# The weighted sum over heads in a prompt indexer: VectorE additions by head, or a second float32 matmul in four column strips

## The chip, the cores and the metric

One Trainium2 chip, one of its cores. The metric is the device time of one execution of the whole program in microseconds (us), the median of several runs. One further execution was taken by the hardware profiler, and all rows below come from it.

## The reference

Two layers of a streaming encoder run on 512 prompt tokens and 32 sample tokens. Each layer projects its normed input with one combined matrix, runs three mixers, an output projection and a feed-forward network. Mixer C is a sparse attention: an indexer scores every key for each query, the best k keys are kept, and attention runs over those. The indexer, cut from the reference:

```python
logits = relu(einsum('bqnd,bsd->bqns', qi, ki_all))
iscore = einsum('bqn,bqns->bqs', wi, logits)
iscore = where(admissible, iscore, -inf)
_, sel = top_k(iscore, k_top)
```

There are n = 8 indexer heads of 32 features. `wi` holds a weight for each query token and head. For the prompt the queries come in blocks of 128 tokens; a block sees the keys up to its own chunk of 64 tokens.

## The kernel before, in words

Features are split over partitions and tokens lie along the free axis, in two halves (256 prompt tokens; 256 prompt and 32 sample tokens). Large products are made exact enough from three float32r products of split operands (`mm3`, L225 to L227). Weights come in by DMA and are split by ScalarE (L216) and VectorE or GpSimd (L217). Some products of the sample's 32 rows are true float32 (L377): eight pieces of the contraction, four of them side by side in strips of 32 columns of the array, which `sum4` (L370) adds up afterwards.

A layer's mixer C begins with the indexer, `for b in range(5)`, L494 to L581. Blocks b = 0 to 3 are the prompt's, b = 4 is the sample. Each block's projection comes from `tok_gemm` (L497); L396, L398 and L509 apply the rotary factors, L508 keeps the eight weights per token in `wi`. The key part is split in two (L516, L518), transposed and appended to `kiTp` (L522). The query part is split (L530, L532), transposed (L103, the one line of all transposes) and copied to `qiT` (L540), so that one matmul of 128 contraction rows gives a head's float32-like scores.

For prompt blocks b = 1 to 3 (n = 256, 384, 512 keys) the loop over heads is:

```python
for hd in range(8):
    pl = psum("lld"[hd % 3])
    nc.tensor.matmul(pl[:, :n], lhsT=qiT[:, hd, :], rhs=kiTp[:, :n], start=True, stop=True)
    rl = T(n, "tt")
    nc.scalar.activation(rl, pl[:, :n], AF.Relu)
    if hd == 0:
        nc.vector.tensor_scalar(work, rl, wi[:, 0:1], None, op0=ALU.mult)
    else:
        nc.vector.scalar_tensor_tensor(work, rl, wi[:, hd:hd + 1], work, op0=ALU.mult, op1=ALU.add)
```

These are L544 (TensorE), L546 (ScalarE), L548 and L550 (VectorE). L551 masks the later chunk. The sample block does the same with a second matmul: L576 gives scores of four heads times 32 tokens, L579 sums them over heads with a float32 matrix `wsel` that L561 and L570 build from `wi`.

Behind the indexer come the q, k and v projections with rotary factors and norms (L597, L622, L641; the key's norm is L644 to L648, its transposes go through L103), the top-k selection of the prompt blocks on VectorE (`topk_mask`, L405 and L406, 16 rounds a block), the search for the sample's threshold (`sample_mask`, L431 to L443) and attention (L689 and on).

The order of each engine is set by a scheduler: instructions have priorities in the order in which they are traced (shifted for weight loads and copies out of PSUM, class `Shift`), and each engine then takes its instructions strictly in the order so found. Gemm matmuls of other products are laid between the indexer's steps in this way; they are called fillers here.

Of the kernel before, what the change touches and what calls it, by code (L numbers as in the profile page):

```python
# [25 lines left out]
# column groups of w_in  # L26
# [5 lines left out]
# scheduling priorities of weight loads and of copies out of PSUM  # L32
PREP = -1000000
EVAC = -2000000
# columns of the ring of split weights
# [3 lines left out]
class Shift:  # L39
    """Shifts the scheduling priority of what is traced inside."""  # L40
# [12 lines left out]
def kernel(  # L53
# [39 lines left out]
    def psum(tag):  # L93
        return pp.tile([128, 512], F32, tag=tag, name=nm("ps" + tag), bufs=PBUFS[tag])
# [4 lines left out]
    def tr(out, in_, ident):  # L99
        """A transpose on TensorE, which moves the bits as they are (float32r in one pass)."""  # L100
        if in_.dtype == F32R:
            out = out.bitcast(F32R)
        nc.tensor.transpose(out, in_, ident)  # L103
# [20 lines left out]
    # per-feature vectors as columns: g_mix, g_ffn, conv_w, state_conv  # L124
# [23 lines left out]
    def rsqrt_newton(r, s, scale, shape_like):  # L148
        """r = (s * scale) ** -0.5, the table's value with one Newton step; s may lie in PSUM."""
# [9 lines left out]
    def take_x(h, tags):  # L159
        """A half of x to feature-major, and the norm's factors along the rows' columns."""  # L160
# [34 lines left out]
    for g in range(4):  # L195
        nc.vector.tensor_copy(sum4[32 * g:32 * g + 32, 96:128], idn[32 * g:32 * g + 32, 32 * g:32 * g + 32])
    p = psum("o")
# [4 lines left out]
    ring = [wp.tile([128, RING], F32R, name="hi"), wp.tile([128, RING], F32R, name="lo"), 0]  # L202

    def load_w(fill, a, c, eng=None):
        """a row blocks of weights, c columns each: two float32r parts that sum to them exactly, and they themselves."""
# [24 lines left out]
    # the sample's normed rows, not split  # L230
    hraw = const.tile([128, 8, 32], F32, name="hraw")

    def add_square(h, m):
        """Adds the squares of block m of x to the half's sum (with the eps share of a partition)."""
# [29 lines left out]
    def results(b, g, tag):  # L264
        """A block's output, half of its features, back to token-major."""
# [15 lines left out]
    def prepare(l):  # L281
# [42 lines left out]
    def search_constants():  # L324
# [3 lines left out]
        # for the threshold search: prefix sums, the copies' total, steps  # L328
# [15 lines left out]
    for l in range(depth):  # L344
# [20 lines left out]
        def tok_gemm(b, pieces, n, aside=True):  # L365
            """Token-major product of a block; aside: the sample's rows by themselves, in float32."""
# [5 lines left out]
            if b == 0 and aside:  # L372
                # the sample's rows: parts of the sum side by side in the array's columns
# [17 lines left out]
        def rope(t1, t2, x, ca, sb, half):  # L391
            """t1 = x * cos, t2 = swapped x * sin; x [rows, j, h, e] in PSUM."""
# [8 lines left out]
        def topk_mask(work, n, rounds, tag):  # L401
            """Turns scores into 0 where taken and NEG elsewhere."""
# [6 lines left out]
        def sample_mask(x):  # L409
            """The same for the sample's scores, whose rows are there four times (rows 32 j + t).  # L410

            The k-th largest score is found digit by digit (two bits of its float's exponent or mantissa at a
            time, each copy of a row trying one digit); equal scores are taken in the order of the keys.
            """
# [4 lines left out]
            # sign of the k-th largest; which one of sgn * x it is  # L419
# [7 lines left out]
            def digit(nb):  # L427
                """How many candidates of a row at least kk of sgn * x reach (a tie at the candidate counts half)."""
# [29 lines left out]
            # a tie at the last candidate may have hidden it: count exactly there  # L458
# [10 lines left out]
            # prefix counts of the equal ones  # L469
# [8 lines left out]
            # as many of them as are missing: k - (sum of signs + n - equal) / 2  # L478
# [15 lines left out]
        for b in range(5):  # L494
# [38 lines left out]
            if b < 4:  # L533
                n = 128 * (b + 1)
                qiT = Q([128, 8, 128], F32R)
                for g in range(2):
                    pt = psum("l")
                    for k in range(4):
                        tr(pt[:, k * 128:k * 128 + 128], qs[:, 4 * g + k].rearrange("p a e -> p (a e)"), idr)
                    nc.scalar.copy(qiT[:, 4 * g:4 * g + 4, :].rearrange("p h t -> p (h t)"), pt)  # L540
                work = keep([128, n], f"work{b}")
                for hd in range(8):
                    pl = psum("lld"[hd % 3])
                    nc.tensor.matmul(pl[:, :n], lhsT=qiT[:, hd, :], rhs=kiTp[:, :n], start=True, stop=True)  # L544
                    rl = T(n, "tt")
                    nc.scalar.activation(rl, pl[:, :n], AF.Relu)  # L546
                    if hd == 0:
                        nc.vector.tensor_scalar(work, rl, wi[:, 0:1], None, op0=ALU.mult)  # L548
                    else:
                        nc.vector.scalar_tensor_tensor(work, rl, wi[:, hd:hd + 1], work, op0=ALU.mult, op1=ALU.add)  # L550
                nc.vector.memset(work[0:64, n - 64:n], INADM)  # L551
                masks[b] = work
            else:
# [5 lines left out]
                # w as two [(head, t), (copy, t)] matrices  # L559
# [47 lines left out]
        for u in range(2):  # L607
            pieces = w_tok(C_Q + 256 * u, 256, ((0, 4), (4, 8)), nc.gpsimd)
            for b in range(5):
# [5 lines left out]
                # columns (j, hh, e) to (hh, j, e)  # L615
# [63 lines left out]
        def attend(b):  # L679
            """The block's steps of a pair of query heads: scores and softmax, then the values."""  # L680
# [3 lines left out]
            def scores(u, hh):  # L684
                # two key heads side by side: their scores in halves of the array's rows
# [21 lines left out]
            def values(u, hh, probs, po):  # L707
                for k0 in range(0, b + 1, 2):
# [7 lines left out]
                    # and their values in halves of its columns  # L716
# [16 lines left out]
        def attend_sample():  # L733
# [17 lines left out]
            # queries, scaled  # L751
# [293 lines left out]
```

## Time and profile before

| what | value |
|---|---|
| median of 3 runs | 1400.68 us (1397.32 to 1401.14) |
| the profiled execution, its span | 1403.4 us |
| TensorE busy | 1353.1 us, 96% |
| VectorE busy | 840.0 us, 60% |
| ScalarE busy | 615.9 us, 44% |
| GpSimd busy | 115.3 us, 8% |

For the profiled execution the page gives the span and no other time. Busy shares are means over the whole span; the windows below show stretches of ten microseconds, in which an engine that is busy for 10.00 has no gap. PE is TensorE, DVE VectorE, ACT ScalarE, POOL GpSimd. In a row of the timeline, "[2.42 <-ACT t L546]" says that the engine was idle for 2.42 us before, and that ScalarE's instruction of line 546, which writes a tile named t, released it. A float32 matmul leaves two records, so that x16 of L377 are eight matmuls. PEclk is the clock that TensorE was granted, 1.00 being full speed.

### The profile page before, as it was taken

The page shows a single profiled execution, that of the slowest core. Times are in us where ns is not written, and L with a number is a line of the kernel's source. Part 1 is how long each engine was busy: PE and PEld are TensorE (multiplying, and loading weights), DVE is VectorE, ACT ScalarE, POOL GpSimd, SP SyncE. Part 2 cuts the span into 40 slices and gives each one's busy share as a digit, 9 for nine tenths or more (in the row PEclk, how much of TensorE's full clock was granted, in tenths as well). Part 3 has the DMA queues.
Part 4 walks back from the last instruction along what each step waited for, and adds up shares of the span by engine and source line. Part 5 has one row for each costly group of instructions (what it writes and reads, how often), then busy time and mean ns, then how long its engine had stood idle before and what let it go on. Part 6 is the DMA issues. An engine that isn't in the chain of part 4 may idle for free. (4 is left out here: it accounts for less than half of the span.)

```text
span 1403.4 us, 25751 instructions
## 1 busy us (share of the span) xinstructions
PE 1353.1 (96%) x10430; PEld 1265.8 (90%) x10430; DVE 840.0 (60%) x2103; ACT 615.9 (44%) x1212; POOL 115.3 (8%) x125
## 2 busy tenths in 40 slices
PE   7998999998999999999989899999899999999998
PEld 5877886898999999999987789779799999999998
DVE  6999987468434334334489999865853343443442
ACT  5746996335314224223246489842542231331321
POOL 4414200010000000000042120000200000000000
PEclk8999999999999999999988999999999999999999
DMA  7124221323233332333212222222233332233322
GB/s 185 33 71 106 68 64 48 94 68 89 81 88 91 91 84 84 89 91 91 64 49 62 58 81 77 76 61 61 61 95 88 91 91 86 82 90 91 91 81 74
DMA packets 183566, 113.00 MB, mean 81 GB/s; under 512 B 7028, under 2 KB 180616, under 8 KB 183448
## 3 DMA queue, kind: packets, MB, share of 16 engines
q1 hardware_dynamic: 180808, 106.35, 26.2%
q0 software_dynamic: 2640, 5.01, 1.8%
q8 instruction: 82, 1.34, 0.4%
q14 instruction: 36, 0.29, 0.1%
HBM read 106.67 MB, written 4.67 MB: 79 GB/s over the span
## 5 line engine op out<-in xcount | busy, mean ns | idle before, releaser
L216 ACT CAST hi<-raw 128x1024 fp32r<-128x1024 f32 (+1 forms) x188 | 194.1, 1032 | 404.6 <-PE psm L226 389.1
L217 DVE TENSOR_TENSOR lo<-raw,hi 128x1024 fp32r<-128x1024 f32 (+1 forms) x163 | 197.5, 1212 | 174.9 <-ACT hi L216 174.2
L908 DVE TENSOR_TENSOR x<-x,psm 128x256 f32<-128x256 f32 (+1 forms) x192 | 83.7, 437 | 232.4 <-PE psm L227 232.0
L226 PE MATMUL psm<-h1lo,hi 128*128 128x288 f32 x640 | 190.4, 298 | 0.9 <-DVE h1lo L222 0.9
L227 PE MATMUL psm<-a1hi,lo 128*128 128x288 f32 x640 | 190.0, 297 | 0.0
L226 PE MATMUL psm<-a1lo,hi 128*128 128x288 f32 x640 | 189.9, 297 | 0.0
L225 PE MATMUL psm<-a1hi,hi 128*128 128x288 f32 x640 | 189.8, 297 | 0.0
L225 PE MATMUL psm<-h1hi,hi 128*128 128x288 f32 x640 | 188.7, 296 | 1.1 <-ACT h1hi L221 1.1
L227 PE MATMUL psm<-h1hi,lo 128*128 128x288 f32 x640 | 189.1, 296 | 0.0
L226 PE MATMUL psm<-h0lo,hi 128*128 128x256 f32 x640 | 181.9, 285 | 6.2 <-DVE h0lo L222 6.2
L225 PE MATMUL psm<-a0hi,hi 128*128 128x256 f32 x640 | 183.0, 286 | 0.0
L226 PE MATMUL psm<-a0lo,hi 128*128 128x256 f32 x640 | 182.0, 284 | 0.0
L227 PE MATMUL psm<-a0hi,lo 128*128 128x256 f32 x640 | 182.0, 284 | 0.0
L225 PE MATMUL psm<-h0hi,hi 128*128 128x256 f32 x640 | 181.4, 284 | 0.0
L227 PE MATMUL psm<-h0hi,lo 128*128 128x256 f32 x640 | 180.0, 282 | 0.0
L226 PEld LDWEIGHTS psm<-h0lo,hi 128*128 128x128 f32 x640 | 120.4, 188 | 8.6 <-DVE h0lo L222 7.1
L225 PEld LDWEIGHTS psm<-h1hi,hi 128*128 128x128 f32 x640 | 120.1, 188 | 2.7 <-ACT h1hi L221 1.5
L225 PEld LDWEIGHTS psm<-a0hi,hi 128*128 128x128 f32 x640 | 121.6, 190 | 0.5 <-issue 0.5
L226 PEld LDWEIGHTS psm<-h1lo,hi 128*128 128x128 f32 x640 | 120.3, 188 | 1.8 <-DVE h1lo L222 1.3
L226 PEld LDWEIGHTS psm<-a0lo,hi 128*128 128x128 f32 x640 | 121.2, 189 | 0.6 <-issue 0.5
L225 PEld LDWEIGHTS psm<-h0hi,hi 128*128 128x128 f32 x640 | 120.6, 189 | 1.2 <-issue 0.9
L227 PEld LDWEIGHTS psm<-a0hi,lo 128*128 128x128 f32 x640 | 121.6, 190 | 0.0
(318 smaller groups left out, 2841.1 us busy)
## 6 DMA issues: line engine op xcount, KB each, us to landing
raw<-in_w_up_dram SPq DMA_DIRECT2D x64, 512.0 KB, 4.1
raw<-in_w_down_dram SPq DMA_DIRECT2D x64, 512.0 KB, 3.9
raw<-in_w_in_dram SPq DMA_DIRECT2D x36, 512.0 KB, 3.9
raw<-in_w_out_dram SPq DMA_DIRECT2D x8, 512.0 KB, 3.8
raw<-in_w_out_dram SPq DMA_DIRECT2D x32, 128.0 KB, 3.0
raw<-in_w_in_dram SPq DMA_DIRECT2D x8, 296.0 KB, 6.1
q<-in_cache_k_dram SPq DMA_DIRECT2D x4, 512.0 KB, 4.3
h1lo<-in_cache_v_dram SPq DMA_DIRECT2D x2, 1024.0 KB, 7.1
```

The lines of the kernel that those rows point to most:

```text
L216: nc.scalar.copy(hi, raw)
L217: (eng or nc.vector).tensor_tensor(lo, raw, hi.bitcast(F32), op=ALU.subtract)
L225: nc.tensor.matmul(out, lhsT=st[0], rhs=mv[0], start=first, stop=False)
L226: nc.tensor.matmul(out, lhsT=st[0], rhs=mv[1], start=False, stop=False)
L227: nc.tensor.matmul(out, lhsT=st[1], rhs=mv[0], start=False, stop=last)
L908: nc.vector.tensor_tensor(xs[h][:, m, :], xs[h][:, m, :], p[:, :HALF[h]], op=ALU.add)
```

## The change

The 128 query tokens of a prompt block are taken as four quarters of 32. A score matmul now has four heads times 32 tokens as its output rows, like the sample's, so there are still eight a block (two groups of heads g, four quarters q4). The weighted sum over heads is a float32 matmul with a 128 × 32 matrix of weights `wst` for each g and q4, which writes the quarter's 32 rows of one PSUM tile (tag "o", one buffer); the two groups accumulate. ScalarE copies the sum to `work`. `wst` is made by GpSimd (weights times a matrix of stacked identities, `fold`), two float32 transposes and a copy. The lines behind move by 5 to 21: L544 becomes L564, L546 L566, L551 L572, L579 L600, L225 to L227 become L230 to L232, L377 L382, L509 L514, L518 L523, L532 L537, L396 L401, L405 L410, L406 L411.

```diff
+    fold = const.tile([128, 32], F32, name="fold")
+    nc.vector.memset(fold, 0.0)
+    for g in range(4):
+        nc.vector.tensor_copy(fold[32 * g:32 * g + 32], idn[32 * g:32 * g + 32, 32 * g:32 * g + 32])
...
-                qiT = Q([128, 8, 128], F32R)
+                qiT = Q([128, 2, 4, 4, 32], F32R)
...
-                    nc.scalar.copy(qiT[:, 4 * g:4 * g + 4, :].rearrange("p h t -> p (h t)"), pt)
+                    nc.scalar.copy(qiT[:, g].rearrange("p q h t -> p h q t"), pt.rearrange("p (h q t) -> p h q t", h=4, q=4))
+
+                dg = T(256)
+                nc.gpsimd.tensor_tensor(
+                    dg.rearrange("p (h t) -> p h t", h=8),
+                    wi.rearrange("p (h o) -> p h o", o=1).to_broadcast([128, 8, 32]),
+                    fold.rearrange("p (o t) -> p o t", o=1).to_broadcast([128, 8, 32]), op=ALU.mult)
+                wst = T(256)
+                pt = psum("l")
+                for g in range(2):
+                    tr(pt[:, g * 128:g * 128 + 128], dg[:, g * 128:g * 128 + 128], idn)
+                nc.scalar.copy(wst, pt[:, :256])
+
                 work = keep([128, n], f"work{b}")
-                for hd in range(8):
-                    pl = psum("lld"[hd % 3])
-                    nc.tensor.matmul(pl[:, :n], lhsT=qiT[:, hd, :], rhs=kiTp[:, :n], start=True, stop=True)
-                    rl = T(n, "tt")
-                    nc.scalar.activation(rl, pl[:, :n], AF.Relu)
-                    if hd == 0:
-                        nc.vector.tensor_scalar(work, rl, wi[:, 0:1], None, op0=ALU.mult)
-                    else:
-                        nc.vector.scalar_tensor_tensor(work, rl, wi[:, hd:hd + 1], work, op0=ALU.mult, op1=ALU.add)
+                pi = psum("o")
+                for g in range(2):
+                    rls = []
+                    for q4 in range(4):
+                        pl = psum("lld"[(4 * g + q4) % 3])
+                        nc.tensor.matmul(pl[:, :n], lhsT=qiT[:, g, q4].rearrange("p h t -> p (h t)"), rhs=kiTp[:, :n], start=True, stop=True)
+                        rl = T(n, ("tt", "tt", "pt", "g")[q4])
+                        nc.scalar.activation(rl, pl[:, :n], AF.Relu)
+                        rls.append(rl)
+                    for q4 in range(4):
+                        c = g * 128 + 32 * q4
+                        nc.tensor.matmul(pi[32 * q4:32 * q4 + 32, :n], lhsT=wst[:, c:c + 32], rhs=rls[q4], start=(g == 0), stop=(g == 1))
+                nc.scalar.copy(work, pi[:, :n])
                 nc.vector.memset(work[0:64, n - 64:n], INADM)
```

The change also moves instructions, since the scheduler sets the order anew. The first place is TensorE in block 1 of layer 0, among the score matmuls (q is `qiT`, psm the gemm's sum). Before:

```order
L225 MATMUL psm_888<-hi,h0hi_184 128x256
L544 MATMUL psl_506<-kiTp_325,q_487 128x256
L226 MATMUL psm_888<-lo,h0hi_184 128x256
L544 MATMUL psl_516<-kiTp_325,q_487 128x256
L227 MATMUL psm_888<-hi,h0lo_185 128x256
L225 MATMUL psm_888<-hi,h0hi_184 128x256
L226 MATMUL psm_888<-lo,h0hi_184 128x256
L544 MATMUL psl_521<-kiTp_325,q_487 128x256
L227 MATMUL psm_888<-hi,h0lo_185 128x256
L225 MATMUL psm_888<-hi,h0hi_184 128x256
```

With the change, from the third score matmul of the block on (pso is the new sum, its t operands are a Relu's output and `wst`):

```order
L564 MATMUL psl_527<-kiTp_331,q_493 128x256
L570 MATMUL pso_514<-t_517,t_508 32x256
L570 MATMUL pso_514<-t_521,t_508 32x256
L570 MATMUL pso_514<-t_525,t_508 32x256
L564 MATMUL psl_535<-kiTp_331,q_493 128x256
L570 MATMUL pso_514<-t_529,t_508 32x256
L564 MATMUL psl_543<-kiTp_331,q_493 128x256
L230 MATMUL psm_921<-hi,h0hi_190 128x256
L231 MATMUL psm_921<-lo,h0hi_190 128x256
L232 MATMUL psm_921<-hi,h0lo_191 128x256
```

Score matmuls and fillers now alternate with the new products, three of which stand together and the fourth behind a further score matmul. The transposes of key block 0 in layer 0, further on, have 31 gemm matmuls between themselves and the transposes ahead of them, where they had 24; in layer 1 both orders have 24.

The second place is VectorE from the sample block's L509 (now L514) on, in layer 0. Before:

```order
L509 TENSOR_TENSOR t_771<-t_771,t_772 32x288
L548 TENSOR_SCALAR work_100_500<-t_503,wi_93_467 128x256
L550 SCALAR_TENSOR_TENSOR work_100_500<-t_508,wi_93_467,work_100_500 128x256
L550 SCALAR_TENSOR_TENSOR work_100_500<-t_513,wi_93_467,work_100_500 128x256
L550 SCALAR_TENSOR_TENSOR work_100_500<-t_518,wi_93_467,work_100_500 128x256
L518 TENSOR_TENSOR ks_576<-t_567,ks_576 128x32 x2
L550 SCALAR_TENSOR_TENSOR work_100_500<-t_523,wi_93_467,work_100_500 128x256
L532 TENSOR_TENSOR q_584<-t_567,q_584 128x8x32
L550 SCALAR_TENSOR_TENSOR work_100_500<-t_528,wi_93_467,work_100_500 128x256
L532 TENSOR_TENSOR q_584<-t_567,q_584 128x8x32
```

With the change:

```order
L514 TENSOR_TENSOR t_804<-t_804,t_805 32x288
L523 TENSOR_TENSOR ks_591<-t_582,ks_591 128x32 x2
L537 TENSOR_TENSOR q_599<-t_582,q_599 128x8x32 x2
L572 MEMSET work_103_513 64x64
L410 MAX m_489_1997<-work_103_513 128x8
L401 TENSOR_TENSOR t_946<-psm_921,tab_76_418 128x2x2x64
L403 TENSOR_TENSOR t_947<-psm_921,tab_77_421 128x2x2x32 x2
L523 TENSOR_TENSOR ks_702<-t_693,ks_702 128x32 x2
L643 TENSOR_TENSOR t_946<-t_946,t_947 128x256
L411 MATCH_REPLACE work_103_513<-m_489_1997,work_103_513 128x256
```

The steps of block 2 (its ks and q) follow the sample's addition at once, and the top-k selection of block 1 (MAX, MATCH_REPLACE) begins here, where before the additions of `work` stand. Where the key's norm begins, block 1 has had 16 rounds of its selection, where it had 7, and block 2 has had 10, where it had 4.

## Rows read from the trace of the kernel before

**Rows 1.** The page, busy time, share of the span and instructions of each engine.

```profile
PE 1353.1 (96%) x10430; PEld 1265.8 (90%) x10430; DVE 840.0 (60%) x2103; ACT 615.9 (44%) x1212; POOL 115.3 (8%) x125
```

**Rows 2.** Windows: each engine's busy us (instructions), TensorE's granted clock, DMA share, GB/s.

```profile
50.00:60.00 10.00, 8.04 (x49) 7.55 (x50) 8.81 (x25) 6.62 (x20) 3.06 (x3) 0.83 0.19 54
60.00:70.00 10.00, 9.88 (x70) 8.80 (x69) 9.22 (x24) 9.08 (x21) 0.00 (x0) 1.00 0.01 2
70.00:80.00 10.00, 8.07 (x55) 5.93 (x54) 9.48 (x21) 3.87 (x11) 2.36 (x1) 0.85 0.33 100
100.00:110.00 10.00, 8.37 (x71) 8.20 (x71) 9.89 (x36) 3.12 (x8) 3.16 (x2) 1.00 0.37 126
110.00:120.00 10.00, 7.60 (x64) 6.48 (x62) 9.91 (x41) 4.39 (x10) 3.96 (x4) 0.90 0.44 133
740.00:750.00 10.00, 8.44 (x57) 8.12 (x57) 9.08 (x20) 7.58 (x22) 3.01 (x3) 0.87 0.36 107
760.00:770.00 10.00, 8.40 (x61) 7.05 (x61) 9.71 (x22) 4.78 (x11) 2.36 (x1) 0.83 0.35 107
790.00:800.00 10.00, 8.00 (x68) 7.82 (x67) 9.93 (x35) 2.88 (x7) 2.95 (x2) 1.00 0.23 66
800.00:810.00 10.00, 7.68 (x62) 6.49 (x61) 9.57 (x40) 4.67 (x10) 3.47 (x3) 0.88 0.46 140
```

**Rows 3.** TensorE's timeline, layer 0: start, us, instruction, [idle before <-releaser].

```profile
51.42 0.39 PE L544 MATMUL psl<-kiTp,q 128*128 128x256 f32 x1 [2.42 <-ACT t L546]
...
73.97 0.98 PE L103 MATMUL psl<-idr,q 32*128 32x32 f32 x10 [1.44 <-ACT t L546]
```

**Rows 4.** TensorE's timeline, layer 1, same columns.

```profile
736.77 0.58 PE L544 MATMUL psl<-kiTp,q 128*128 128x256 f32 x1 [2.04 <-ACT q L540]
...
737.74 1.94 PE L377 MATMUL psm<-raw,hraw 128*32 128x256 f32 x16
...
766.29 0.31 PE L103 MATMUL psl<-idr,q 32*128 32x32 f32 x2 [1.11 <-DVE q L561]
```

**Rows 5.** All engines' timeline, 47.8 to 51.0 us, same columns.

```profile
47.80 2.38 POOL L217 TENSOR_TENSOR lo<-raw,hi 128x1024 fp32r<-128x1024 f32 x1
...
47.93 2.57 DVE L509 TENSOR_TENSOR t<-t,t 32x288 f32<-32x288 f32 x1
...
50.98 0.39 ACT L546 ACTIVATE t<-psl 128x256 f32<-128x256 f32 x1 [2.58 <-DVE work L548]
```

**Rows 6.** VectorE's instructions by line: count, busy us, mean ns, idle before.

```profile
L550 DVE SCALAR_TENSOR_TENSOR work<-t,wi,work 128x256 f32<-128x256 f32 (+2 forms) x42 | 31.3, 746 | 1.3 <-DVE wsel L570 0.3
...
L548 DVE TENSOR_SCALAR work<-t,wi 128x256 f32<-128x256 f32 (+2 forms) x6 | 2.4, 396 | 0.1
```

**Rows 7.** Waits of TensorE: total us, times, longest us.

```profile
PE psx L103 <- DVE sr L644: 3.6, 2, 2.0
```

**Rows 8.** TensorE's timeline, 111.9 to 113.8 us.

```profile
111.93 0.28 PE L227 MATMUL psm<-hi,h1lo 128*128 128x256 f32 x1
112.05 0.38 PE L103 MATMUL psx<-idr,t 128*128 128x128 f32 x2
112.27 0.60 PE L370 MATMUL psm<-t,sum 128*128 128x256 f32 x2
112.79 1.07 PE L377 MATMUL psm<-raw,hraw 128*32 128x256 f32 x16
113.80 0.18 PE L433 MATMUL psd<-ti,rsum 128*128 128x1 bf16 x1
```

**Rows 9.** TensorE's timeline, 770.3 to 771.4 us: the sample's indexer.

```profile
770.29 1.02 PE L579 MATMUL psl<-t,wsel 128*128 128x512 f32 x2
770.75 0.80 PE L576 MATMUL psl<-kiTs,new 128*128 128x512 f32 x1
771.38 0.38 PE L103 MATMUL psd<-idr,t 128*128 128x128 f32 x2
```

**Rows 10.** ScalarE's Relus of the indexer by line (three widths).

```profile
L546 ACT ACTIVATE t<-psl 128x256 f32<-128x256 f32 (+2 forms) x36 | 17.4, 503 | 5.4 <-DVE work L548 2.6 <-DVE work L550 2.1 <-PE psl L544 0.5
```

**Rows 11.** GpSimd's instructions by line and form.

```profile
L292 POOL TENSOR_TENSOR tab<-tab,t 128x320 f32<-128x320 f32 x8 | 7.5, 931 | 11.1 <-DMA t<-in_k_gain_dram 4.9 <-DMA tab<-in_c_cq_dram 3.5 <-DMA t<-in_q_gain_dram 2.6
```

## Prediction

> **What bounds the kernel now.** I read the page's totals first: TensorE is busy for 96% of the span, VectorE for 60% [rows 1]. A change that only takes work from VectorE can then gain no more than the idle time of TensorE that this work causes, and the lower clock that follows it. So I went on to the windows of ten microseconds in which TensorE is not full [rows 2]. There are two clusters in each layer: the indexer (50 to 80 us, 740 to 770 us), where the change is, and the norm of the keys behind it (100 to 120 us, 790 to 810 us). VectorE is busy for 8.8 to 9.9 of ten microseconds in all of them, so in these stretches it is VectorE that TensorE follows. Everywhere else TensorE has no gap to give back, and each added matmul there is added time. Third, TensorE's timeline shows what a gap in the indexer waits for [rows 3, 4], and the engines together show where one of them begins [rows 5].
>
> **What is removed.** The 42 additions by head (L550) take 31.3 us of VectorE and the six L548 2.4 us [rows 6], about 34 us or 17 a layer. None of it lies on the path by itself. It is there through score tiles that come free late. At 51.42 us a score matmul (L544) waits 2.42 us for a Relu [rows 3]; the Relu waited 2.58 us for the weighted addition of head 0, which stood on VectorE behind an addition of 2.57 us that ran beside GpSimd's weight split L217 of 2.38 us [rows 5]. With the change no score tile is read by VectorE, so these waits go: 2.42 us and 1.44 us in layer 0 [rows 3], and 1.11 us in layer 1 [rows 4], where the transposes of the sample's weights wait for their product L561, which VectorE has among the L550s of block 3. Together 5.0 us. I keep the 2.04 us of layer 1 [rows 4]: it waits for the copy of the queries, which comes before any L550.
>
> A gap also costs clock. The granted clock is 0.83, 0.85 and 0.83 in 50–60, 70–80 and 760–770 us [rows 2]; as the time in these windows that is missing against 1.0 this is 1.7 + 1.5 + 1.7 = 4.9 us, which I take as given back with the gaps ahead of them. The 0.87 of 740–750 us stays, since the gap at 736.77 us ahead of it stays.
>
> Last, the transposes of the key's block 0 wait for its norm (L644), 3.6 us in both layers [rows 7]. In layer 0 the order has 31 gemm matmuls ahead of them where it had 24; in layer 1 it has 24 as before. Seven at 0.12 us (the pitch of a gemm's 256 columns [rows 8]) fill 0.8 us. Removed in all: 5.0 + 4.9 + 0.8 = 10.7 us.
>
> **What is added on TensorE.** The score matmuls keep their number and columns, so they cost nothing more. New are eight float32 products (L570 of the changed kernel) a block, four per group side by side in column strips of 32. The nearest rows are those of L377, which also puts four float32 products of 256 columns side by side: 16 records (two a product) are two groups of four, and the next instruction starts 1.01 us later [rows 8], so 0.50 us a run of up to four. For 512 columns the sample's full-width float32 product has 1.09 us from 770.29 to 771.38 us together with one of its score matmuls (L576) between [rows 9], whose 512 columns I take at twice the 0.12 us that a gemm's 256 take: 0.85 us. For 384 columns I take the middle, 0.68 us.
>
> A run pays its columns once, and only products that stand next to each other form one. The order shows for block 1 of layer 0 runs of three and one, twice, with score matmuls or gemms between. Over the blocks there are 4 + 4 + 4 runs in layer 0 and 4 + 4 + 3 in layer 1, where all four together would need two a block. Sum: 4 × (0.50 + 0.68 + 0.85) = 8.1 us, and 2.0 + 2.7 + 2.6 = 7.3 us: 15.4 us. For the range alone I let each of the 23 runs cost one gemm's pitch more, about 0.1 us [rows 8], 2.3 us, since none of my rows has strips and full matmuls in such quick alternation.
>
> The Trainium skill (TensorEngine Tiling (Array Packing), "Key Properties") speaks against this alternation: tiles run in parallel, but a change of the tiling mode drains TensorE. The row of L377 holds one such change for two groups, and the order has one for each run and one back. The page gives no duration; with 0.1 us a run the sum would be 1410.8 us in place of 1408.5 us, still the same case.
>
> Twelve float32 transposes of the weights come on top (two a block). The pair at 112.05 us holds TensorE for 0.22 us [rows 8]: six pairs, 1.3 us. In layer 1 the first block's runs fall into the stretch behind the gap of 2.04 us that stays; at that clock 16 L377 took 1.94 instead of 1.07 us [rows 4, 8], 0.81 more of each microsecond, so its four runs and its pair of transposes (2.2 us) cost 1.8 us more. Added in all: 15.4 + 1.3 + 1.8 = 18.5 us.
>
> **What costs nothing.** ScalarE gets two copies a block (weights, result), 0.4 to 0.6 us each by its Relus of the same width (mean 0.50 [rows 10]), about 3 us a layer: covered where it is busy for 3 to 8 of ten microseconds, not at 60–70 us, where it is at 9.08 [rows 2] (a rival below). GpSimd multiplies the weights into strips, six times, by the nearest row 0.93 us each [rows 11], in front of which TensorE has gemms; if it collides with VectorE as L217 does, it takes up to 5.6 us of the 34 that VectorE gains. The table of identities built at the start is five short VectorE instructions beside loads. In the order VectorE has 16 rounds of block 1's selection and 10 of block 2's ahead of the first key norm, where it had 7 and 4; that lead is worth something only if it closes the later gaps (first rival).
>
> **Sum.** 18.5 − 10.7 = +7.8 us. The profiled execution spans 1403.4 us, the median of the runs is 1400.7 us, 0.2% below; I put the difference on the median: **1408.5 us**. The bounds: with only two runs a block (8.1 us in all) and the transposes 1.3 us, against all idle time of the indexer's windows (1.96 + 1.93 + 1.56 + 1.60 = 7.1 us), its lost clock (4.9 + 1.3) and the 0.8 us, it is −4.7 us, 1396.0 us. With the mode changes (2.3 us) and no gain from clock or the later turn (5.7 us) it is +15.8 us, 1416.5 us.
>
> **The rivals.** *VectorE's lead closes the later gaps too (faster).* In 100–120 and 790–810 us TensorE lacks 1.63 + 2.40 + 2.00 + 2.32 = 8.35 us and a clock of 0.90 and 0.88 costs 2.2 us [rows 2]. If 17 us less of VectorE work a layer clear all that and every gap of the indexer, 7.1 + 6.2 + 8.35 + 2.2 = 23.9 us go, against 18.5: −5.4 us, 1395 us, and with the runs merged to two a block (7.3 us less) 1388 us. For it: VectorE is full in just these windows. Against it: the order puts the selection of blocks 1 and 2 around the key's norm as densely as before, so VectorE is as full there. It decides once the removed gaps exceed 18.5 us.
>
> *TensorE waits for the Relus it now consumes.* Before, no matmul of a prompt block read a Relu's output; now each group's fourth product does, and in the order only a few instructions stand between its score matmul and it. TensorE takes its work in order, so gemms behind wait too. One mean Relu of 0.50 us [rows 10] for each of 12 groups is 6.1 us, and the clock stays low (4.9 us): 7.8 + 6.1 + 4.9 = +18.8 us, 1419 us. For it: ScalarE's 9.08 at 60–70 us. Against: the scheduler put three products or a gemm into most of these places.
>
> *The strips do not run side by side.* Then each of the 48 products pays its own columns, four times the 8.1 us of two runs a block, 32.4 us instead of 15.4: +24.8 us, 1425 us. Against: L377 does the same thing and does overlap [rows 8].
>
> **Chances.** The forecast 0.50 (its own range 1402 to 1415); the first rival 0.25; waits on Relus 0.18; strips in series 0.04; another way 0.03. A measurement of this kernel tells 0.3%, 4.2 us, from no change. Below 1396.5 us lie somewhat over half of the first rival and a little else: faster 0.22. Between 1396.5 and 1404.9 us lie the rest of that rival and the lower edge of the forecast: same 0.22. Slower 0.56. The range leaves out the faster end of the first rival, the strips in series and part of the Relu waits: 1393 to 1420 us.
>
> **What would show it.** TensorE busy time up by 15 to 20 us while VectorE's falls by about 34; runs of three L570 that take about as long as one product; no wait of a score matmul on a Relu of 2 us; a clock near 1.0 in 50–80 us; gaps at the key's norm that remain, in layer 0 about a microsecond shorter. It is wrong if the later gaps vanish (first rival), or if L570 shows waits on ScalarE in most groups (second).

## The result, and the profile after

The changed kernel takes 1419.72 us (median of 4 runs, 1418.68 to 1420.80), the kernel before 1400.91 us in the same comparison: a ratio of 1.0139, 95% interval 1.0120 to 1.0159. It is 18.8 us slower. The forecast had the direction, and its range (1393 to 1420 us) holds the time at its very edge, but the effect that it named is 7.8 us.

The page's totals, as in [rows 1]:

```profile
PE 1373.0 (97%) x10536; PEld 1266.2 (89%) x10538; DVE 806.8 (57%) x2060; ACT 618.8 (44%) x1222; POOL 117.4 (8%) x131
```

TensorE is busy for 19.9 us more, VectorE for 33.2 us less, as the forecast's last part had it (15 to 20 us and 34 us). Yet the span grew from 1403.4 to 1418.2 us, by 14.8 us and not by 18.8. Most of the rest lies ahead of the indexer's first score matmul: it starts at 45.4 us in the profiled execution of the kernel before, at 41.9 us in that of the changed one, and between 41.3 and 44.5 us in all those of the experiments. The profiled execution of before was a long one: its span alone, 1403.4 us, exceeds the whole time of every timed run (at most 1401.35 us).

The windows of the changed kernel that answer to [rows 2], and two behind them (columns as there):

```profile
50.00:60.00 10.00, 10.00 (x64) 6.11 (x62) 6.76 (x25) 6.54 (x19) 2.25 (x2) 1.00 0.00 0
60.00:70.00 10.00, 9.97 (x48) 5.14 (x47) 7.98 (x27) 7.28 (x18) 0.00 (x0) 1.00 0.01 2
70.00:80.00 10.00, 9.94 (x56) 6.85 (x55) 6.93 (x28) 3.96 (x9) 0.00 (x0) 1.00 0.00 0
100.00:110.00 10.00, 9.83 (x81) 9.63 (x81) 9.87 (x36) 4.32 (x9) 3.53 (x3) 1.00 0.44 139
110.00:120.00 10.00, 7.43 (x64) 6.04 (x64) 8.12 (x39) 4.01 (x9) 3.61 (x3) 1.00 0.30 92
740.00:750.00 10.00, 10.00 (x64) 5.54 (x64) 3.72 (x10) 6.89 (x18) 5.07 (x5) 0.83 0.39 110
760.00:770.00 10.00, 10.00 (x52) 5.37 (x52) 6.46 (x26) 7.00 (x17) 0.00 (x0) 1.00 0.01 2
810.00:820.00 10.00, 6.30 (x57) 4.95 (x55) 6.85 (x28) 4.13 (x8) 3.67 (x3) 0.93 0.41 120
820.00:830.00 10.00, 10.00 (x66) 10.00 (x65) 9.55 (x35) 7.58 (x16) 1.99 (x5) 0.73 0.15 52
```

In the indexer (50 to 80, 760 to 770 us) TensorE is full, at clock 1.00, while VectorE has room: the gaps that the change was to close are closed. At the norm of the keys in layer 0 (100 to 120 us) TensorE lacks 2.74 us where it lacked 4.03 us: about the microsecond that the forecast named. In 740–750 us the clock is 0.83, behind a gap at the start of the block, as before; it is now 3.11 us and stands ahead of the query transposes, which wait for VectorE's split of the queries (L537). At 810–820 us, behind the indexer, TensorE is busy for 6.30 of ten microseconds, less than it was in any window of [rows 2], and VectorE, too, has gaps there (6.85).

TensorE's timeline of block 1 in layer 0 (start, us, instruction; x6 are three products side by side and x2 is one):

```profile
45.24 0.28 PE L564 MATMUL psl<-kiTp,q 128*128 128x256 f32 x1
45.45 0.63 PE L570 MATMUL pso<-t,t 128*32 128x256 f32 x6
46.01 0.39 PE L564 MATMUL psl<-kiTp,q 128*128 128x256 f32 x1
46.33 0.62 PE L570 MATMUL pso<-t,t 128*32 128x256 f32 x2
46.88 0.39 PE L564 MATMUL psl<-kiTp,q 128*128 128x256 f32 x1
47.10 0.28 PE L230 MATMUL psm<-hi,h0hi 128*128 128x256 f32 x1
```

Three products take 0.56 us from their first start to the next instruction, and a single one 0.55 us: the strips do run side by side, and a run costs the same whether it holds one product or three. But it costs more than that. The score matmul ahead of a run has a pitch of 0.21 us (45.24 to 45.45) and not of the 0.12 us that a gemm of 256 columns has, and the one behind it 0.22 us (46.88 to 47.10). The weight loads of the same stretch:

```profile
45.12 0.19 PEld L564 LDWEIGHTS psl<-kiTp,q 128*128 128x128 f32 x1
45.45 0.15 PEld L570 LDWEIGHTS pso<-t,t 128*32 128x32 f32 x6
46.01 0.19 PEld L564 LDWEIGHTS psl<-kiTp,q 128*128 128x128 f32 x1 [0.41 <-issue]
```

The score matmul at 45.24 us has its weights loaded from 45.12 us on, beside the matmul ahead of it. The first strips' weights are loaded only when the run begins (45.45 us), and those of the score matmul behind the run only when it is over (46.01 us).

The same view in block 3, one run of four products:

```profile
63.20 0.41 PE L564 MATMUL psl<-kiTp,q 128*128 128x512 f32 x1
63.54 1.80 PE L570 MATMUL pso<-t,t 128*32 128x512 f32 x8
65.27 0.72 PE L564 MATMUL psl<-kiTp,q 128*128 128x512 f32 x2
```

These four take 1.73 us where a single one of 512 columns takes 0.98 us (68.51 to 69.49 us): the run begins with products whose Relus are done and waits inside for the last one's. TensorE's matmul row shows no idle time there. The row of its weight loads does, and over the whole kernel there are five such waits (columns as in [rows 7]):

```profile
64.29 0.14 PEld L570 LDWEIGHTS pso<-t,t 128*32 128x32 f32 x2 [0.55 <-ACT t L566]
...
PEld pso L570 <- ACT t L566: 2.1, 5, 0.7
```

Behind the indexer, all engines in layer 1 (idle time and what ended it in brackets):

```profile
811.26 0.42 DVE L669 TENSOR_TENSOR t<-t,sr 128x256 f32<-128x256 f32 x1
811.26 2.99 POOL L222 TENSOR_TENSOR lo<-raw,hi 128x1024 fp32r<-128x1024 f32 x1 [2.27 <-ACT hi L221]
...
814.20 0.56 POOL L671 DMA_DIRECT2D out_dram<-t  x1
...
818.64 0.49 DVE L403 TENSOR_TENSOR t<-psm,tab 128x128 f32<-128x128 f32 x2 [3.12 <-DMA out_dram<-t]
...
819.59 0.69 PE L103 MATMUL psx<-idr,t 128*128 128x128 f32 x2 [3.70 <-DVE t L669]
```

VectorE has a block's new keys ready at 811.68 us (L669). GpSimd is at a weight split L222 (2.99 us), and the store of the keys (L671) stands behind it: it is issued at 814.20 us, and lands 4.41 us after that. VectorE's next rotary step (L403) waits 3.12 us for the tile that this store still holds, and TensorE's transposes of the keys wait 3.70 us for VectorE. No part of the forecast has this wait. In the kernel before, none on such a store exceeds 0.4 us in this stretch.

### The profile page after: what moved, and what is told of

It is laid out like the page before. It is cut to its first block, busy times and chain, and to the rows that moved or that the text cites. A ratio compares the mean times of both kernels' runs of the same rounds, so it can differ in the third digit from the quotient of the medians.

```text
span 1418.2 us, 25920 instructions
## 1 busy us (share of the span) xinstructions
PE 1373.0 (97%) x10536; PEld 1266.2 (89%) x10538; DVE 806.8 (57%) x2060; ACT 618.8 (44%) x1222; POOL 117.4 (8%) x131
## 5 line engine op out<-in xcount | busy, mean ns | idle before, releaser
L222 DVE TENSOR_TENSOR lo<-raw,hi 128x1024 fp32r<-128x1024 f32 (+1 forms) x163 | 197.5, 1212 | 180.3 <-ACT hi L221 179.7
L230 PE MATMUL psm<-h1hi,hi 128*128 128x288 f32 x640 | 189.6, 298 | 1.1 <-ACT h1hi L226 1.1
L232 PE MATMUL psm<-a1hi,lo 128*128 128x288 f32 x640 | 190.1, 297 | 0.0
L230 PE MATMUL psm<-a1hi,hi 128*128 128x288 f32 x640 | 189.9, 297 | 0.0
L232 PE MATMUL psm<-h1hi,lo 128*128 128x288 f32 x640 | 189.4, 296 | 0.0
L230 PE MATMUL psm<-h0hi,hi 128*128 128x256 f32 x640 | 183.1, 287 | 0.0
L230 PE MATMUL psm<-a0hi,hi 128*128 128x256 f32 x640 | 183.0, 286 | 0.0
L232 PE MATMUL psm<-a0hi,lo 128*128 128x256 f32 x640 | 182.1, 285 | 0.0
L232 PE MATMUL psm<-h0hi,lo 128*128 128x256 f32 x640 | 181.8, 285 | 0.0
L222 POOL TENSOR_TENSOR lo<-raw,hi 128x1024 fp32r<-128x1024 f32 (+1 forms) x25 | 58.8, 2351 | 789.5 <-ACT hi L221 402.8
L230 PEld LDWEIGHTS psm<-h0hi,hi 128*128 128x128 f32 x640 | 122.2, 191 | 1.6 <-issue 1.2
L232 PEld LDWEIGHTS psm<-h0hi,lo 128*128 128x128 f32 x640 | 121.9, 191 | 1.3 <-issue 1.2
L230 PEld LDWEIGHTS psm<-h1hi,hi 128*128 128x128 f32 x640 | 120.2, 188 | 2.2 <-ACT h1hi L226 1.5
L230 PEld LDWEIGHTS psm<-a0hi,hi 128*128 128x128 f32 x640 | 121.7, 190 | 0.5 <-issue 0.5
```

The lines of the kernel that those rows point to most:

```text
L222: (eng or nc.vector).tensor_tensor(lo, raw, hi.bitcast(F32), op=ALU.subtract)
L230: nc.tensor.matmul(out, lhsT=st[0], rhs=mv[0], start=first, stop=False)
L232: nc.tensor.matmul(out, lhsT=st[1], rhs=mv[0], start=False, stop=last)
```

## The experiments

All times are medians, in microseconds. Experiments 1 to 4, 5 to 8, 9 to 11 and 12 were taken on four chips, and each ratio is to runs of the kernel before on the same chip (1400.5, 1400.3, 1400.5 and 1399.0 us). By their intervals most of these ratios are known to 2 to 4 us, and a difference between two experiments is no better known than that. "Relief" is used for what TensorE gets back because VectorE no longer adds by head.

**1. No weighted sum.** Score and Relu stay, the products, the weight strips and their transposes go.

```diff
-                dg = T(256)
-                nc.gpsimd.tensor_tensor(
...
-                        nc.tensor.matmul(pi[32 * q4:32 * q4 + 32, :n], lhsT=wst[:, c:c + 32], rhs=rls[q4], start=(g == 0), stop=(g == 1))
-                nc.scalar.copy(work, pi[:, :n])
+                nc.scalar.copy(work, rls[3])
```

> The changed kernel without its weighted sum: no products L570, no weight strips, no transposes of them; the score of a prompt block is a copy of one Relu's tile, so the sum over heads is left out. VectorE still does no addition by head. Theory one (the products cost what the forecast said): the changed kernel's time less 15.4 us for 23 runs and 1.3 us for the transposes, about 1403 us. Theory two (the trace of the changed kernel: 20.4 us for the runs themselves and some 4 us for the matmuls before and behind each run, plus 1.4 us of transposes): about 26 us less, 1394 us; the gaps behind the indexer stay. Theory three (the later gaps come from the later indexer, not from the order): 1389 us or less, no gap over 1 us at the key's norm.

1387.8 us (ratio to before 0.9903, 0.9875 to 0.9932): 31.9 us below the changed kernel, more than the first two theories had. Relief is real: without the sum the kernel is 12.7 us below the one before. The sum costs more than twice that. The third theory's time came, but not its sign: gaps of 1.5 to 1.7 us at the key's norm are still there in both layers.

**2. Fewer runs of products.** A later priority for the products.

```diff
-                    for q4 in range(4):
...
+                    with Shift(tc, 800):
+                        for q4 in range(4):
...
```

> The changed kernel with the products given a later priority, so that TensorE's order has 14 runs of L570 (five and three, five and three, one and four and three in each layer) where it had 23. The computation is the same. Theory one (a run costs 0.50, 0.68, 0.85 us and no change of mode): 6.1 us a layer against 7.7, about 3 us less, 1416 us. Theory two (0.55, 0.76, 0.98 us and about 0.25 us at the two ends of a run): 8.7 us a layer against 13, about 8.7 us less, 1411 us. The selection on VectorE begins later by some microseconds, which could give a part back in the stretch of the key's norm.

1413.1 us (ratio 1.0078, 1.0054 to 1.0103): 6.6 us less for nine runs fewer. That is nearer to the second theory (8.7 us) than to the first (3 us).

**3. Key stores on SyncE's queue.**

```diff
-                nc.gpsimd.dma_start(nk_p[l, 0, b * 128:b * 128 + 128].rearrange("t h e -> t (h e)"), kf)
+                nc.sync.dma_start(nk_p[l, 0, b * 128:b * 128 + 128].rearrange("t h e -> t (h e)"), kf)
```

> The changed kernel with the stores of the prompt's new keys (L671) issued by SyncE's queue and not by GpSimd's; runs of L570 unchanged at 23. Theory two (the later gaps come from these stores, which stand on GpSimd behind a weight split L222 and so free VectorE's rotary tiles late: VectorE waited 1.27 and 3.12 us for them, TensorE 0.87 and 3.70 us): both waits go, and with them the low clock behind the second, 4 to 6 us less, about 1414.5 us. Rival (VectorE's work around the key's norm sets the gaps): within 1.5 us of the changed kernel, the gaps move to another instruction of VectorE.

1412.8 us (ratio 1.0084, 1.0059 to 1.0109): 6.9 us less. TensorE's transposes that waited 3.70 us, here:

```profile
818.26 0.44 PE L103 MATMUL psx<-idr,t 128*128 128x128 f32 x2 [0.53 <-DVE t L669]
```

and the two windows in which the changed kernel was busy for 6.30 us at clock 0.93 and then ran at 0.73:

```profile
810.00:820.00 10.00, 9.47 (x85) 8.12 (x84) 9.94 (x43) 5.25 (x11) 3.21 (x2) 1.00 0.50 147
820.00:830.00 10.00, 9.61 (x78) 8.63 (x76) 9.63 (x30) 8.84 (x20) 2.48 (x5) 1.00 0.18 66
```

TensorE's gemm matmuls come in the same order in both kernels, so their traces can be laid side by side. The matmul that starts at 813.7 us in the changed kernel starts 1.25 us later in experiment 3, and the one that starts at 828.2 us starts 4.52 us earlier: 5.8 us gained at this wait, by the gap and the low clock behind it. Over the whole attention, up to 951 us, it is 7.4 us. In layer 0 the store's wait went too, but other waits on VectorE took its place, and nothing was gained there (experiment 3 is behind by 1.8 us at 47 us and by 2.1 us at 303 us).

The edit does two things at once. In experiment 3 the store of these keys is issued 0.02 us after they are ready and lands 1.74 us later, where in the changed kernel it is issued 2.5 us after and lands 4.41 us later (the eight key stores of that kernel take 1.97 to 4.51 us to land). By these rows the wait of 3.12 us would have been some 0.6 us without the place behind the split, and some 1.2 us with a landing of the median 2.5 us: an estimate, and no run separates the two.

**4. The kernel before with more Relu tiles.**

```diff
-                    rl = T(n, "tt")
+                    rl = T(n, ("tt", "tt", "pt", "g")[hd % 4])
```

> The kernel before, additions by head on VectorE unchanged, but with the Relu's tiles taken in turn from the four tags that the change uses (nine buffers where there were four). If the waits of score matmuls on Relus (2.42, 1.44 and 1.56 us) only come from too few tiles, these go with the lower clock behind them, and the time is 5 to 9 us below the kernel before, 1392 to 1396 us, with no product on TensorE at all. If they come from VectorE being behind for good in this stretch, the waits move to the next thing that VectorE owes TensorE (the split query parts, L532) and the time is within 3 us of 1400.9 us.

1402.4 us (ratio 1.0014, 1.0003 to 1.0025). The waits on Relus are gone and the time is not. All engines around the place of the first of them, in layer 0:

```profile
48.06 4.41 DVE L550 SCALAR_TENSOR_TENSOR work<-t,wi,work 128x256 f32<-128x256 f32 x4
...
48.67 2.34 POOL L217 TENSOR_TENSOR lo<-raw,hi 128x1024 fp32r<-128x1024 f32 x1 [0.30 <-ACT hi L216]
...
52.82 0.34 PE L103 MATMUL psl<-idr,ks 128*128 128x128 f32 x1 [4.43 <-DVE ks L518]
...
52.96 0.54 PE L227 MATMUL psm<-hi,h0lo 128*128 128x256 f32 x1
```

Four additions by head take 4.41 us beside a weight split of GpSimd, and TensorE waits 4.43 us for the split of the keys (L518) that stands behind them. So it was VectorE's lateness that cost, not the tiles: the term of the forecast that rests on it holds.

**5 and 6. Full-width products in float32r,** without strips, in one pass; in 6 with the stores of experiment 3.

```diff
-                wst = T(256)
+                if b == 1:
+                    wful = keep([128, SK], "works", F32R)
+                    nc.vector.memset(wful.bitcast(F32), 0.0)
...
-                        rl = T(n, ("tt", "tt", "pt", "g")[q4])
+                        tag = ("tt", "tt", "pt", "g")[q4]
+                        rl = tp.tile([128, n], F32R, tag=tag, name=nm("t"), bufs=TBUFS[tag])
...
-                        c = g * 128 + 32 * q4
-                        nc.tensor.matmul(pi[32 * q4:32 * q4 + 32, :n], lhsT=wst[:, c:c + 32], rhs=rls[q4], start=(g == 0), stop=(g == 1))
+                        c = (4 * g + q4) * 128
+                        nc.tensor.matmul(pi[:, :n], lhsT=wful[:, c:c + 128], rhs=rls[q4], start=(g + q4 == 0), stop=(g + q4 == 4))
```

> The weighted sum as full-width products: weights in eight 128 x 128 matrices that are zero outside a quarter's columns, and weights and Relus rounded to float32r, so that a product takes one pass and no strips are used. The precision of the sum over heads is lower than before. Theory two (the price of the change is passes plus the changes between strips and full matmuls): 48 products at the pitches of the score matmuls (0.12, 0.17, 0.23 us, 8.4 us in all) on top of the kernel without the sum, 1387.8 us, and 1.4 us of transposes: 1397.6 us, and the matmuls next to the products keep their pitch. Rival (the price is mostly the new dependence of TensorE on the Relus, whatever a product costs): 1410 us or more, with waits on ScalarE before these products.

> The same with the stores of the prompt's new keys on SyncE's queue. If the store's place on GpSimd's queue costs 4 to 7 us whenever VectorE gets to the key's norm early: 1391 to 1394 us, below the kernel before. If it cost the changed kernel so much only because of where its stores fell: within 2 us of the same kernel without this edit.

1407.3 us (ratio 1.0052, 1.0035 to 1.0068) and 1398.1 us (ratio 0.9987, 0.9970 to 1.0004). In 6 a product and its neighbours keep the pitch of 0.12 us:

```profile
44.68 0.28 PE L568 MATMUL psl<-kiTp,q 128*128 128x256 f32 x1
44.80 0.28 PE L575 MATMUL pso<-t,works 128*128 128x256 f32 x1
44.92 0.28 PE L230 MATMUL psm<-hi,h0hi 128*128 128x256 f32 x1
45.04 0.28 PE L231 MATMUL psm<-lo,h0hi 128*128 128x256 f32 x1
```

So it isn't the new dependence on the Relus that costs. But 5 is 10 us above the 1397.6 us that was expected, and neither forecast for 6 came (1391 to 1394 us, or within 2 us of 5): the edit takes 9.2 us off. What it takes off is not shown. In the trace of 5 VectorE's longest wait for a key store is 0.45 us, and TensorE's gaps at the key's norm (2.08, 1.78, 1.91 and 1.75 us) wait for steps of that norm on VectorE and not for a store.

**7. Fewer runs and stores on SyncE's queue.**

> The changed kernel with 14 runs of products instead of 23 and with the key stores on SyncE's queue, both earlier edits at once. If they act on different places (the runs in the indexer, the stores behind it): 1419.7 - 6.6 - 7.0 = 1406 us. If the later start of the selection already moved the stores out of GpSimd's way: no more than 1 us below the 1413.1 us of the fewer runs alone.

1403.8 us (ratio 1.0021, 1.0003 to 1.0039). The two edits add up: 9.0 us for the runs with the stores out of play (1412.8 to 1403.8), where the prices of experiment 2 had 8.7 us. In the traces the time within the runs falls from 20.4 to 13.4 us; the ends of nine runs come on top. The agreement to 0.3 us is closer than either time is known.

**8. The kernel before with its stores on SyncE's queue.**

> The kernel before with nothing changed but the key stores on SyncE's queue. VectorE waited 0.34 us for one of them there, and TensorE for none: if the cost of the stores belongs to the change's timing, the time is within 1.5 us of 1400.5 us; if they cost every version the same, it is 4 to 7 us less, 1395 us.

1400.2 us (ratio 0.9998, 0.9980 to 1.0016): nothing. The cost of the stores is not in the kernel before; it came with the change.

**9. No weighted sum, stores on SyncE's queue.**

> The changed kernel without its weighted sum over heads (left out as in the first experiment) and with the key stores on SyncE's queue: what VectorE's relief is worth by itself. Together with the changed kernel with its stores on SyncE (1412.8 us) it gives the price of the weighted sum without the stores in play. By the trace of the changed kernel that price is 20.4 us of runs, some 4 us at their ends and 1.4 us of transposes, so about 1387 us; the same as without the store edit (1387.8 us). If the first experiment also paid for late stores (it shows gaps of 1.74 us behind VectorE's L654 in both layers), 1381 to 1384 us, and the price is 29 us or more.

1387.2 us (ratio 0.9901, 0.9875 to 0.9926). The first case: with the stores out of play on both sides, the weighted sum costs 1412.8 − 1387.2 = 25.6 us, and relief is 13.3 us (10 to 18 us by the interval). Beside experiment 1 the store edit is worth 0.6 us: VectorE's work is moved here too, so that alone does not make the stores costly. Experiment 6 agrees with the price of a product without strips: beside the kernel before it is 11.1 us above this one (−2.2 and −13.3 us), where 48 products and the transposes had been put at 8.4 + 1.4 us.

The traces give a somewhat smaller price. From 9 to 3 the span grows by 25.3 us, of which 2.4 us lie ahead of the first score matmul (41.29 and 43.72 us): 22.9 us.

**10 and 11. A search for a version below both.** Experiment 6 with the indexer keys' stores on SyncE's queue as well (10), and with the strips' weights made by VectorE (11).

> Full-width float32r products, key stores on SyncE's queue, and the indexer keys' stores (L516) there too. In the kernel with the first two edits VectorE waited 1.32 us for an indexer key's store in layer 1, and its next split was blocked for 2.88 us beside a weight split, with a gap of 3.11 us on TensorE. If that store is the cause: 3 to 5 us below 1398.1 us, 1394 us, clearly below the kernel before. If the weight split alone is: within 1.5 us of 1398.1 us.

> The same with the weights' strips made by VectorE and not by GpSimd. GpSimd's multiplication took 0.63 to 0.66 us, and 2.55 us beside VectorE's work. If GpSimd's added work matters for when its splits and VectorE's meet, 1 to 3 us below the kernel with all stores on SyncE; if not, the same within 1.5 us, since VectorE pays about 0.4 us for each of the six.

1400.2 us (ratio 0.9994, 0.9982 to 1.0006) and 1400.4 us (ratio 1.0001, 0.9986 to 1.0017). Neither helps; in 10 the gap of 3.11 us became gaps of 0.84 and 1.65 us. The lowest with a sum over heads is experiment 6, 2.2 us below the kernel before, which its interval does not tell from no change. It rounds the weights and the Relus to float32r, so its sum over heads is less precise.

**12. Full-width products in float32.** As 6, with float32 weights and Relus.

> Full-width products again, but in float32: 48 products of 128 output columns, zero outside a quarter's, key stores on SyncE's queue. The result is the changed kernel's. It tells what the ends of a run come from and what the strips are worth. At the prices of single runs in the changed kernel (0.55, 0.76, 0.98 us) 48 products take 36.6 us. If the 0.1 us before and behind a run comes from going from full matmuls to strips and back, it is gone here: 1387.2 + 36.6 + 1.4 = 1425 us. If it comes from going from float32r to float32, it stays at the ends of each run: 3 to 6 us more, 1430 us, and the matmul next to a full-width float32 product shows it. If the strips had been no better than products in series, the time would be that of the changed kernel with its stores on SyncE, 1413 us.

1423.0 us (ratio 1.0179, 1.0147 to 1.0211), near the 1425 us of the first case, though in part by luck (below). TensorE's timeline and its weight loads around the first four products:

```profile
45.88 0.28 PE L568 MATMUL psl<-kiTp,q 128*128 128x256 f32 x1
45.89 0.31 PEld L575 LDWEIGHTS pso<-t,works 128*128 128x128 f32 x2
46.01 1.96 PE L575 MATMUL pso<-t,works 128*128 128x256 f32 x8
...
47.59 0.19 PEld L568 LDWEIGHTS psl<-kiTp,q 128*128 128x128 f32 x1
47.62 0.47 PE L568 MATMUL psl<-kiTp,q 128*128 128x256 f32 x1
...
47.92 0.28 PE L568 MATMUL psd<-kiTp,q 128*128 128x256 f32 x1
```

The run takes 1.61 us and the score matmul behind it 0.30 us; less that one's own 0.12 us, this is 1.79 us for four products, 0.45 us each. The score matmul ahead of them keeps its 0.12 us, and their first weights are loaded from 45.89 us on, 0.12 us ahead of the product; behind the run the next weights begin 0.03 us ahead. Over the other runs the pitches give 0.43, 0.64 and 0.86 us for 256, 384 and 512 columns, the first score matmul behind a run included; the matmul ahead of a run loses 0 to 0.1 us. A single strip product with its ends costs 0.55 + 0.09 + 0.10 = 0.74, about 0.96 and about 1.18 us: some 0.3 us more than the columns at every width, of which full-width float32 shows no more than 0.1 us.

At these prices 48 full-width products cost 16 × (0.43 + 0.64 + 0.86) = 30.9 us and not the 36.6 us of the expectation, which had taken the strips' 0.55, 0.76 and 0.98 us for columns. The sum is then 1419.5 us, and some 3.5 us of the 1423.0 us are not accounted for.

## Why the prediction was right in its direction and wrong in its size

**Relief: right.** The forecast took 10.7 us off for waits, clock and the later turn; experiment 9 has 13.3 us, and the windows of the indexer show it. It kept the gap at the start of the indexer of layer 1, and there is still one. It left one wait out, which is of the same kind as those that it took off; in the kernel before, layer 1:

```profile
749.74 0.44 PE L544 MATMUL psd<-kiTp,q 128*128 128x384 f32 x1 [1.56 <-ACT t L546]
```

This is all the idle time of 740–750 us [rows 2], and with the change the window is full.

**The price of a run: mis-sized.** This is the first step that failed: "so 0.50 us a run of up to four", read from two groups of L377 that stand next to each other [rows 8], and with it "For the range alone I let each of the 23 runs cost one gemm's pitch more". By experiment 12 the columns of a float32 product of 256 cost 0.43 us; L377's 1.01 us holds two of them and 0.15 us besides, and nothing of what the neighbours lose. Halving it left each run 0.07 us of ends, where a short run pays 0.31 us (0.74 less 0.43). The rest of that step follows in the same way: 0.68 and 0.85 us hold no end at all. The price, with the stores out of play, was 25.6 us against the forecast's 18.5 us. It adds up from the trace: columns 4 × (0.43 + 0.64 + 0.86) + 4 × 0.43 + 4 × 0.64 + 3 × 0.86 = 14.6 us; 23 ends of 0.3 us, 6.9 us; the waits inside five runs for the last Relu, 3.0 us in all (by how much each exceeds a single run; the weight loads' row has 2.1 us of it); transposes about 1.4 us: 25.9 us. That this meets the 25.6 us so closely is luck in part: the traces of 9 and 3 differ by 22.9 us, so in these traces some 3 us of the sum are regained elsewhere. The 1.8 us for cold products in layer 1 were not needed, since block 1's products came when the clock was up again.

The Trainium skill (TensorEngine Tiling (Array Packing), "Key Properties") has the rule that was weighed and left out of the sum: a change of the tiling mode drains TensorE. The runs agree: the ends appear with strips and not with full-width float32 products, and the strips' first weights are loaded only when the run begins, where those of the full-width products are loaded 0.12 us ahead. The page has no duration; here going into strips and back costs 0.2 to 0.3 us, which the forecast had put at 0.1 us and in the range alone.

**The wait for the stores: not seen.** The second step that failed is the one on VectorE's lead ("that lead is worth something only if it closes the later gaps"), together with what it says of GpSimd. In layer 1 the lead was not merely worth nothing: a gap opened, where the rotary step of the keys met a store that was queued behind a weight split. This is 6.9 us (experiment 3), and it is not the same in every version: nothing in the kernel before, 0.6 us without the sum, 9.2 us in the full-width version, where the trace doesn't show by what. What I left out is that a store holds its tile until it has landed: here 2.5 us behind GpSimd's split and 4.41 us on its way.

**Together:** 25.6 − 13.3 + 6.9 = +19.2 us, against the 18.8 us measured. This sum closes by itself, since its three terms are the differences along one chain of medians (before, 9, 3, changed): it divides the effect, and does not test the division. Against the forecast's 7.8 us, the price is 7.1 us more, the stores 6.9 us more, and relief 2.6 us better.

**The rivals.** The first (the later gaps go) is ruled out: TensorE lacks 3.70 us in 810–820 us where it lacked 2.32 us in 800–810 us [rows 2], and 2.74 us remain in layer 0. The second (waits on the Relus) gave 1419 us, which is the time that came, for another reason: it had 6.1 us of waits (twelve times 0.50 us are 6.0) and a clock that stays low; 3.0 us of such waits are there, in five of the twelve groups and inside the runs, and the clock is 1.00 in the indexer of layer 0. The third (strips in series) is ruled out by three products in 0.56 us. Experiment 12 shows what it would have been: 1423.0 us for full-width products in series, 10 us above strips with the same stores.

**What stays open.** Why moving the indexer keys' stores, too, gave nothing (experiment 10) was not settled, nor what the key stores' edit takes off the full-width version. Whether the ends of a run come from a drain of the whole array or from the weight loads that do not go ahead is not separated either. Fewer than 14 runs of products were not tried. And attention in layer 0 has a gap that the kernel before does not have, for which no run was made:

```profile
138.41 0.70 PE L710 MATMUL psl<-kTp,qT 64*128 64x128 f32 x4 [2.12 <-DVE sa L717]
```

It is there in experiment 3 too (2.51 us), so it is not the key stores.

## What to carry to other kernels

A price that is read from a group of like matmuls holds its ends only once, and what the neighbours lose not at all; before it is divided by the number of groups, the pitch of the neighbours ahead and behind has to be looked at, and the new order has to be counted in runs, not in products. When an engine is relieved, follow every buffer that it takes over from a store: the store's place on its queue and the time that it takes to land decide when the buffer is free, and a store queued behind long work on GpSimd can undo a gain elsewhere. And a version with the whole suspected cost left out (here 13 us of relief against 26 us of price) shows in one run about how much a cheaper form of the change could win.

## What was not expected of the hardware

The same two gaps of TensorE, 1.28 and 1.83 us at the head of the feed-forward, sometimes cost clock and sometimes not. In the changed kernel, layer 0 (columns as in [rows 2]):

```profile
319.00:323.00 4.00, 2.48 (x17) 2.13 (x17) 4.00 (x7) 1.49 (x3) 2.53 (x1) 1.00 0.45 131
323.00:327.00 4.00, 3.38 (x16) 3.38 (x17) 3.90 (x11) 2.92 (x8) 0.00 (x0) 0.59 0.49 135
```

and in the kernel before, with gaps of the same length:

```profile
316.00:320.00 4.00, 2.49 (x17) 2.15 (x17) 4.00 (x7) 1.64 (x3) 2.53 (x1) 1.00 0.46 131
320.00:324.00 4.00, 3.09 (x25) 3.10 (x26) 3.90 (x12) 3.08 (x9) 0.00 (x0) 1.00 0.45 131
```

The clock fell to a mean of 0.59 in one, and stayed at 1.00 in the other. From the first norm matmul of that stretch to the second it is 16.6 us in the one case and 15.3 us in the other. There are 28 such stretches, two in each of the fourteen profiled executions, and the same code runs in all: 13 are near 16.6 us and 15 between 15.3 and 15.7 us, and five executions have one of each. With one profiled execution a version it can't be told whether the version or chance decides.

It bears on the result: the kernel before has 15.3 us in both layers and the changed kernel 16.6 us in both, so 2.6 of the 14.8 us between their two spans lie here, far from the change. How much of it is in the medians is not known. A difference of less than 3 us between two versions may be this and nothing else.
